# One DiT layer on one core: the array fed during the first loads, S5's two directions in one scan, and an order with a place for each instruction

## The chip, the core and the metric

The kernel runs on one core of a Trainium2 chip: TensorE (PE, with its weight loads as PEld), VectorE (DVE), ScalarE (ACT), GpSimd (POOL) and the queue that issues the transfers (SP) each work through their own list of instructions in order, and wait on each other through semaphores. The metric is the device time of one execution in microseconds; lower is better.

## The reference, cut to what matters

One layer over 512 latent tokens and a prefix of 256 context tokens, 1024 channels, all float32.

```
h   = rms_norm(x) * (1 + scale) + shift        # scale, shift, gate from silu(c) @ W_ada
prj = h @ W_in     # q,k,v | GLA q,k,v,gates | S5 input (256) | three merge gates (3 x 1024)
A = bidirectional gated linear attention, chunks of 64 tokens
B = bidirectional S5: 16 groups of 16 channels, 64 complex states each
    state_t = a * state_{t-1} + B u_t, once forward in time and once backward; y = Re(C state) + D u
C = grouped-query softmax attention, 4 heads over context + latent keys
m = sum_i sigmoid(gate_i) * (branch_i @ W_br_i);  x += gate * (m @ W_out)
x += gate2 * ffn(rms_norm(x) * (1 + scale2) + shift2)    # 2816 wide, width-3 convolution
```

## The kernel before

Everything is recorded first and ordered afterwards. A class `Sched` stands in for the engines: each call (`PE.matmul`, `V.tensor_tensor`, `SY.dma_start`) is recorded as an operation with its cost in a model, its predecessors, and the name of the part that was current (`part("s5z0")`). `prepare` gives every operation a rank: the longest chain behind it, but at least the number that the table `WANT` has for its part. `forward` then walks through model time and gives each engine, whenever it is free, the ready operation of the highest rank. `emit` writes the real instructions in that order, so one line number stands for all of them (L408). What the chip does with the list is then fixed: an engine whose next instruction has to wait holds up everything behind it. Copies recorded on `VS` or `VG` may be placed on DVE or on ACT or POOL, as the planner finds room.

Float32 products are taken as three passes over split operands (`hh`/`hl` high and low part of the normalised input, `wbgh`/`wbgl` of a weight), hence three matmuls of 128x512 for each tile. The casts that make the parts run on ACT, DVE and POOL.

The stages, in the order of time. **Start**: 12 matmuls of ones (`warm`); the input in 8 tiles `xT`; their mean square (`rl`); and for each of 8 blocks of channels k a `modulation(k)`: 2 tiles `ada` of 512 KB, 8 matmuls that fill a quarter of the array's columns each, a copy `adar`, 2 small matmuls, then scale and shift, from which `hh`, `hl` are made. **b1**: the projection of block k as soon as its `hh` stands (`b1a`, `b1c`). `low` is the projection to GLA's gates (`tp<-hh,wgl`, 96x512). **S5**: the 16 groups in four quarters q; each turns its input (`uT`, copied to `U`), multiplies it into the state space (`Z`), rotates it by tables `co`, `si` (`zt`, `z`), scans along 512 columns (`so`), rotates back (`x_`) and multiplies into `y`. The rows of `Z` from 0 to 63 are forward states, 64 to 127 backward states; the scan runs left to right on the first half and right to left on the second, as two instructions:

```python
V.tensor_tensor_scan(xo[0:64, 1:512], df[0:64, 0:511], zf[0:64, 0:511], 0.0, ...)
V.tensor_tensor_scan(xo[64:128, 0:511][:, ::-1], df[64:128, 1:512][:, ::-1], zf[64:128, 1:512][:, ::-1], 0.0, ...)
```

**Attention** (`sc`, `sl` scores; `sm` their maximum; `Pc`, `Pl` exponentials; `pt`, `ptc` transposes; `oatt`), **GLA** (`tp`, `kvE`, `kvO`, `ba`, `bo`), **output and residual** (`tk`, `h2T`) and the **FFN** (`up`, `tk`) follow. Two sorts of work are free to stand nearly anywhere from b1 to the residual: the merge gates `bg` (576 matmuls of 128x512, whose weights come in 24 tiles `wbg`) and the branch outputs `br`. The planner lays them where PE would otherwise wait.

Of the kernel before, what the change touches and what calls it, by code (L numbers as in the profile page):

```python
# [15 lines left out]
ALU = mybir.AluOpType  # L16
# [12 lines left out]
NWARM = 12  # L29
WHOLE = ("mm8t",)  # L30
# [4 lines left out]
SHARE = 0.97  # L35
WANT = {
# [87 lines left out]


class _Op:
    __slots__ = ("i", "alts", "acc", "succ", "npred", "news", "fset", "mcost", "part", "pe", "port")


class Sched:  # L130
# [1791 lines left out]
```

## Time and profile before

| what | value |
|---|---|
| median of 3 runs | 942.54 us (935.72 to 943.57) |
| the profiled execution | 944.47 us, of which 942.7 us are its span |
| PE busy | 887.6 us, 94% |
| DVE, ACT, POOL busy | 606.6, 376.7, 169.8 us |
| moved by DMA | 107.67 MB, 114 GB/s on the mean |

Times in the trace are microseconds from the start of the span. A stretch in which PE is busy at a granted clock of 1.0 is at full speed; at 0.5 the same matmuls take twice as long and PE still counts as busy. So the busy share alone doesn't say where time is lost: the granted clock is read beside it.

### The profile page before, as it was taken

Reading aid. Unit: us, or ns where it says so; the run is one execution under the profiler, and the core shown is the slowest. Engines: PE = TensorE matmul, PEld = TensorE weight load, DVE = VectorE, ACT = ScalarE, POOL = GpSimd, SP = SyncE. Lnnn points to the kernel's source line nnn. Section 1 sums busy time; section 2 is a strip of 40 time slices with the busy share of each in tenths; the row PEclk is TensorE's granted clock in tenths of the full one; section 3 lists DMA queues with packets and bytes.
Section 4 is the critical chain, followed back from the end, with each engine's and each line's share of the span. In section 5 each row is a group of like instructions: output and inputs, shape, how many; then the busy total and the mean of one; then the engine's idle time right before and its main releaser. Section 6 shows DMA issues by size and latency. Waiting matters only on the chain.

```text
span 942.7 us, 12225 instructions
## 1 busy us (share of the span) xinstructions
PE 887.6 (94%) x4552; PEld 716.3 (76%) x4552; DVE 606.6 (64%) x1151; ACT 376.7 (40%) x710; POOL 169.8 (18%) x132
## 2 busy tenths in 40 slices
PE   6999986789999999999899989999999999999996
PEld 4597864567777888778788767888888888888885
DVE  7679789987768432495644787454575546956314
ACT  4445154355754633244364375122232223722001
POOL 2310020003221432167056402110100100100000
PEclk7599996889999999999999997999999999999999
DMA  9715112140224322356447312222232222443101
GB/s 339 296 62 180 50 50 66 52 165 25 89 68 143 112 67 90 113 200 201 146 166 257 129 34 81 87 90 67 90 126 98 90 67 85 162 147 128 60 23 68
DMA packets 39644, 107.67 MB, mean 114 GB/s; under 512 B 7214, under 2 KB 10942, under 8 KB 39584
## 3 DMA queue, kind: packets, MB, share of 16 engines
q1 hardware_dynamic: 39584, 106.88, 33.5%
q8 instruction: 36, 0.59, 0.3%
q14 instruction: 24, 0.20, 0.1%
HBM read 103.49 MB, written 3.38 MB: 113 GB/s over the span
## 4 chain that ended last, share of the span: by engine, by line
PE 49%; DVE 5%; DMA 1%; issue 1%; ACT 0%; DVEq 0%; SPq 0%
PE up L408 26%; PE tk L408 15%; PE bg L408 4%; PE br L408 2%; PE tp L408 1%; DVE so L408 1%; DMA wbg<-in_wbg 1%; DVE x L408 1%; DVE tmp L408 0%; DMA ada<-in_ada 0%; PE bo L408 0%; DVE rsx L408 0%; DVE y L408 0%; DVE ml L408 0%; DVE rsy L408 0%
## 5 line engine op out<-in xcount | busy, mean ns | idle before, releaser
L408 PE MATMUL up<-h2h,wuph 128*128 128x512 f32 (+1 forms) x384 | 118.5, 377 | 2.5 <-ACT h2h L408 2.5
L408 PE MATMUL up<-h2h,wupl 128*128 128x512 f32 (+1 forms) x384 | 114.5, 374 | 0.0
L408 PE MATMUL up<-h2l,wuph 128*128 128x512 f32 (+1 forms) x384 | 114.5, 375 | 0.0
L408 PE MATMUL bg<-hh,wbgh 128*128 128x512 f32 x192 | 79.2, 425 | 9.5 <-ACT wbgh L408 5.6
L408 PEld LDWEIGHTS up<-h2h,wuph 128*128 128x128 f32 x384 | 70.6, 190 | 17.0 <-ACT h2h L408 3.2
L408 PEld LDWEIGHTS up<-h2h,wupl 128*128 128x128 f32 x384 | 70.5, 189 | 14.5 <-DVE wupl L408 0.5
L408 PEld LDWEIGHTS up<-h2l,wuph 128*128 128x128 f32 x384 | 70.5, 190 | 12.6 <-POOL h2l L408 0.2
L408 PE MATMUL bg<-hh,wbgl 128*128 128x512 f32 x192 | 77.8, 421 | 1.1 <-DVE wbgl L408 1.1
L408 PE MATMUL bg<-hl,wbgh 128*128 128x512 f32 x192 | 77.7, 418 | 0.0
L408 ACT CAST wuph<-wup 128x1024 fp32r<-128x1024 f32 x26 | 27.4, 1054 | 119.1 <-PE up L408 106.2
L408 DVE CAST wuph<-wup 128x1024 fp32r<-128x1024 f32 x18 | 11.9, 691 | 82.4 <-PE up L408 80.1
L408 DVE SCALAR_TENSOR_TENSOR u<-up,col,u 128x511 f32<-128x511 f32 x88 | 60.0, 742 | 3.8 <-ACT u L408 3.6
L408 POOL TENSOR_TENSOR wupl<-wup,wuph 128x1024 fp32r<-128x1024 f32 x9 | 21.6, 2407 | 215.2 <-ACT wuph L408 169.1
L408 POOL TENSOR_TENSOR j<-ada,cbc 128x1024 f32<-128x1024 f32 x16 | 39.6, 2483 | 101.4 <-DMA ada<-in_ada 39.4
L408 PEld LDWEIGHTS bg<-hh,wbgh 128*128 128x128 f32 x192 | 38.0, 198 | 21.0 <-ACT wbgh L408 7.5
L408 PE MATMUL tk<-wtkl,gh 128*128 128x512 f32 x176 | 51.5, 390 | 0.0
L408 PE MATMUL tk<-wtkh,gh 128*128 128x512 f32 x176 | 51.5, 389 | 0.0
L408 PE MATMUL tk<-wtkh,gl 128*128 128x512 f32 x176 | 51.4, 389 | 0.0
L408 DVE TENSOR_TENSOR wupl<-wup,wuph 128x1024 fp32r<-128x1024 f32 x35 | 41.1, 1219 | 15.7 <-PE up L408 14.5
L408 PEld LDWEIGHTS bg<-hh,wbgl 128*128 128x128 f32 x192 | 37.2, 194 | 11.2 <-DVE wbgl L408 2.3
L408 DVE TENSOR_TENSOR wtkl<-wtk,wtkh 128x1024 fp32r<-128x1024 f32 x22 | 26.6, 1221 | 28.4 <-PE tk L408 13.9
L408 PEld LDWEIGHTS bg<-hl,wbgh 128*128 128x128 f32 x192 | 37.4, 195 | 8.9 <-issue 0.5
(483 smaller groups left out, 2009.9 us busy)
## 6 DMA issues: line engine op xcount, KB each, us to landing
ada<-in_ada SPq DMA_DIRECT2D x48, 512.0 KB, 4.9
wup<-in_wup SPq DMA_DIRECT2D x44, 512.0 KB, 3.5
wbg<-in_wbg SPq DMA_DIRECT2D x24, 512.0 KB, 4.4
wtk<-in_wdn SPq DMA_DIRECT2D x22, 512.0 KB, 5.1
wP<-in_wP SPq DMA_DIRECT2D x16, 512.0 KB, 4.0
wbr<-in_wbr SPq DMA_DIRECT2D x8, 512.0 KB
wo<-in_wout SPq DMA_DIRECT2D x16, 256.0 KB, 4.2
w<-in_wB SPq DMA_DIRECT2D x8, 384.0 KB, 7.8
```

Source lines behind the costliest of these rows:

```text
L408: r = getattr(self.real[e], m)(*a, **k)
```

## The change

Three things. (1) Before each of the first loads is used, PE multiplies it by ones: 2 matmuls of 128x128 on each of the 8 `xT` tiles and 1 on each `ada` tile of the first two blocks, 20 in all, into an accumulator that nobody reads. All `modulation(k)` are recorded ahead of the loop over `h`. (2) S5's backward direction gets its input in reversed order of the columns (`R`, two more copies for each quarter), so both directions run left to right: 64 `Z` matmuls in two halves of the columns instead of 32 whole ones, one scan of 128 rows instead of two of 64, and `x_` is put together in two halves, the second written in reverse. (3) `WANT` has a number for each instruction of a part (in units of 50 ns) where it had one for the part, and the rank of an operation is held to its own number; the rule that gave all of a part `mm8t` one rank is gone, and some constants of the model are other ones.

```diff
-NWARM = 12
-WHOLE = ("mm8t",)
+NWARM, NWX, NWA, KWA = 12, 2, 1, 2
...
 WANT = {
-    "": -540.5, "start": -775.6, "warm": 1508.5, "xT": -852.4, "ada0": 973.9, "h0": 896.3, "b10": 763.6, "ada1": 897,
...
+    "h0": [2038, 1563, 1399],
...
 def prepare(self):
-            r = self.want.get(o.part, 0.0) * 1000.0
+            at = self.want.get(o.part)
+            r = -50.0 * at[o.k] if at else 0.0
...
-        top = {}
-        for o in ops:
-            if o.part.startswith(WHOLE):
-                top[o.part] = max(top.get(o.part, 0.0), rank[o.i])
-        return [top.get(o.part, rank[o.i]) for o in ops]
+        return rank
...
-    part("warm")
-    b = ps("warm")
-    for _ in range(NWARM):
-        PE.matmul(b[:, 0:P], lhsT=onesm, rhs=onesm, start=True, stop=True)
+    accA = [ps("b1a") for _ in range(4)]
+    accC = [ps("b1c") for _ in range(2)]
+
+    def warm(src, n):
+
+        at, sc.part_ = sc.part_, "warm"
+        for _ in range(n):
+            PE.matmul(accC[1][:, 0:P], lhsT=onesm, rhs=src[:, 0:P], start=True, stop=True)
+        sc.part_ = at
+
+    warm(onesm, NWARM)
...
         SY.dma_start(t, A["xT"][k])
         xT.append(t)
+        warm(t, NWX)
...
             SY.dma_start(w, A["ada0"][k, i])
+            if k < KWA:
+                warm(w, NWA)
...
+    for k in range(KT):
+        modulation(k)
     for k in range(KT):
         part(f"h{k}")
         hi, lo = g2("hh", dt=F32R), g2("hl", dt=F32R)
-        modulation(k)
-        part(f"h{k}")
...
         VS.copy(U[:, :, 96:128], b3[:, :, 0:32])
+        R = g2("R", [P, 4, 128])
+        VS.copy(R[:, :, 32:128], b3[:, :, 0:96][:, :, ::-1])
+        VS.copy(R[:, :, 0:32], b3[:, :, 0:32][:, :, ::-1])
...
-                PE.matmul(b[:, j * P:j * P + P], lhsT=pT[i][:, j * P:j * P + P], rhs=U[:, j, :], start=True, stop=True)
+                for d, x in enumerate((U, R)):
+                    PE.matmul(b[64 * d:64 * d + 64, j * P:j * P + P], lhsT=pT[i][:, j * P + 64 * d:j * P + 64 * d + 64],
+                              rhs=x[:, j, :], start=True, stop=True)
...
-            V.tensor_tensor_scan(xo[0:64, 1:512], df[0:64, 0:511], zf[0:64, 0:511], 0.0, op0=ALU.mult, op1=ALU.add)
-            V.tensor_tensor_scan(xo[64:128, 0:511][:, ::-1], df[64:128, 1:512][:, ::-1], zf[64:128, 1:512][:, ::-1],
-                                 0.0, op0=ALU.mult, op1=ALU.add)
+            V.tensor_tensor_scan(xo[:, 1:512], df[:, 0:511], zf[:, 0:511], 0.0, op0=ALU.mult, op1=ALU.add)
...
-            if i == 0:
-                mul(x_, so[0], cl)
-                mul(x2, so[1], sl)
-                sub(x_, x_, x2)
...
+            mul(x1, so[0], (cl, sl)[i])
+            mul(x2, so[1], (sl, cl)[i])
+            (sub, add)[i](x_[0:64], x1[0:64], x2[0:64])
+            (sub, add)[i](x_[64:128, :, ::-1], x1[64:128], x2[64:128])
...
-    c["kidx"] = np.where(dirn == 0, s, 127 - s)
-    c["kmask"] = np.where(dirn == 0, s != 0, s != 127)
+    c["kidx"] = s + 0 * dirn
+    c["kmask"] = (s != 0) + 0 * dirn
```

The order that comes out of the new table differs nearly everywhere. Three places show it. In these lists a name ends in a buffer's number, shapes are those of what is written, and x4 is four in a row.

On PE at the start, before: the modulation's matmuls stand in a row, and the projection `b1a` of block 0 follows them.

```order
L408 MATMUL ada_161<-ada_95_162,cpad_75 32x256 x4
L408 MATMUL ada_161<-ada_96_163,cpad_75 32x256 x4
L408 MATMUL ada_171<-ada_105_172,cpad_75 32x256 x4
L408 MATMUL ada_161<-cst_68,adar_164 128x2 x2
L408 MATMUL ada_171<-ada_106_173,cpad_75 32x256 x4
L408 MATMUL ada_180<-ada_114_181,cpad_75 32x256 x4
L408 MATMUL ada_171<-cst_68,adar_174 128x2 x2
L408 MATMUL b1a_106<-w1h_119,hh_112 128x512
L408 MATMUL b1a_108<-w1h_119,hh_112 128x512
L408 MATMUL b1c_110<-w1h_119,hh_112 128x256
```

On PE at the start, changed: the same matmuls, and `low` (`tp_233`) of the blocks already normalised between them.

```order
L919 MATMUL tp_233<-hh_148,wglh_231 96x512
L919 MATMUL ada_123<-ada_58_125,cpad_75 32x256 x4
L919 MATMUL ada_127<-ada_62_129,cpad_75 32x256 x4
L919 MATMUL ada_123<-cst_68,adar_126 128x2 x2
L919 MATMUL tp_233<-hl_149,wglh_231 96x512
L919 MATMUL tp_233<-hh_148,wgll_232 96x512
L919 MATMUL ada_127<-cst_68,adar_130 128x2 x2
L919 MATMUL tp_233<-hh_154,wglh_231 96x512
L919 MATMUL tp_233<-hl_155,wglh_231 96x512
L919 MATMUL tp_233<-hh_154,wgll_232 96x512
L919 MATMUL ada_131<-ada_66_133,cpad_75 32x256 x4
```

What moved: 19 of the 24 matmuls of `low` now stand ahead of the first `b1a` and the other five just behind it; before they stood around the `Z` of S5's second quarter, together with the context's 24 of 96x256, which have left S5 too.

On DVE in S5's second quarter, before (the scan is listed as SCALAR_TENSOR_TENSOR): two rotations, four scans, and `x_` in three steps for each half of the complex number.

```order
L408 TENSOR_TENSOR zt_359<-zt_359,z_289_361 128x512
L408 TENSOR_TENSOR zt_358<-zt_358,z_288_360 128x512
L408 SCALAR_TENSOR_TENSOR so_291_363<-d_283_355,zt_359 64x511
L408 SCALAR_TENSOR_TENSOR so_290_362<-d_283_355,zt_358 64x511 x2
L408 SCALAR_TENSOR_TENSOR so_291_363<-d_283_355,zt_359 64x511
L408 TENSOR_TENSOR x__292_364<-so_290_362,co_354 128x256
L408 TENSOR_TENSOR x_293_365<-so_291_363,si_353 128x256
L408 TENSOR_TENSOR x__294_366<-so_290_362,si_353 128x256
L408 TENSOR_TENSOR x__292_364<-x__292_364,x_293_365 128x256
L408 TENSOR_TENSOR x_295_367<-so_291_363,co_354 128x256
```

On DVE at the same place, changed.

```order
L919 TENSOR_TENSOR zt_362<-zt_362,z_292_364 128x512
L919 TENSOR_TENSOR zt_361<-zt_361,z_291_363 128x512
L919 SCALAR_TENSOR_TENSOR so_294_366<-d_286_358,zt_362 128x511
L919 SCALAR_TENSOR_TENSOR so_293_365<-d_286_358,zt_361 128x511
L919 TENSOR_TENSOR x_297_369<-so_294_366,si_356 128x256
L919 TENSOR_TENSOR x_296_368<-so_293_365,co_357 128x256
L919 TENSOR_TENSOR x__295_367<-x_296_368,x_297_369 64x256
L919 TENSOR_TENSOR x__295_367<-x_296_368,x_297_369 64x4x64
```

What moved: two scans of 128 rows stand where four of 64 rows stood; and each `x_` is written by two instructions of 64 rows.

On PE in the attention, before: scores with the merge gates `bg` between them.

```order
L408 MATMUL sc_578<-kTc_507,qT_505 128x256 x4
L408 MATMUL sl_581<-kTl_506,qT_505 128x512
L408 MATMUL sl_582<-kTl_506,qT_505 128x512
L408 MATMUL bg_652<-hl_132,wbgh_650 128x512
L408 MATMUL sl_581<-kTl_506,qT_505 128x512
L408 MATMUL sl_582<-kTl_506,qT_505 128x512
L408 MATMUL bg_652<-hh_131,wbgl_651 128x512
L408 MATMUL bg_652<-hh_140,wbgh_650 128x512
L408 MATMUL bg_652<-hl_141,wbgh_650 128x512
```

On PE in the attention, changed.

```order
L919 MATMUL sc_578<-kTc_518,qT_516 128x256 x4
L919 MATMUL br_490<-ol_465,wbrh_472 128x512
L919 MATMUL br_490<-oh_464,wbrl_473 128x512
L919 MATMUL pt_574<-cst_68,Pl_573 128x128 x3
L919 MATMUL ptc_566<-cst_68,Pc_561 128x128 x4
L919 MATMUL pt_576<-cst_68,Pl_575 128x128 x4
L919 MATMUL pt_565<-cst_68,Pl_564 128x128 x2
L919 MATMUL sl_592<-kTl_517,qT_516 128x512 x2
L919 MATMUL sl_593<-kTl_517,qT_516 128x512 x2
L919 MATMUL br_515<-oh_462,wbrh_497 128x512
L919 MATMUL br_515<-ol_463,wbrh_497 128x512
L919 MATMUL br_515<-oh_462,wbrl_498 128x512
```

What moved: the branch outputs `br` stay, but the `bg` are mostly gone from here. Of the 576 matmuls of `bg`, the list before has 56 ahead of S5's first `uT`, 143 from there to its last `y`, 185 in the attention, none up to GLA's first `kvO`, and 192 behind it; the changed list has 48, 264, 48, 48 and 168 at the same places.

## Rows read from the trace of the kernel before

**Rows 1.** The page: busy time, share and instructions of each engine.
```profile
PE 887.6 (94%) x4552; PEld 716.3 (76%) x4552; DVE 606.6 (64%) x1151; ACT 376.7 (40%) x710; POOL 169.8 (18%) x132
```

**Rows 2.** Stretches: start:end, length, busy (count) by engine, clock, DMA share, GB/s.
```profile
12.00:26.00 14.00, 8.46 (x44) 5.43 (x44) 13.26 (x42) 7.02 (x11) 2.06 (x3) 0.50 1.03 408
26.00:41.00 15.00, 13.47 (x98) 6.82 (x97) 9.46 (x23) 6.63 (x13) 4.21 (x10) 0.50 0.96 371
...
103.60:206.60 103.00, 81.02 (x467) 61.28 (x466) 94.36 (x158) 43.32 (x74) 6.53 (x7) 0.84 0.27 83
206.60:324.00 117.40, 116.41 (x633) 91.36 (x631) 86.51 (x188) 72.28 (x160) 28.40 (x26) 1.00 0.24 79
...
393.50:477.00 83.50, 76.49 (x484) 63.12 (x480) 61.56 (x147) 33.72 (x81) 37.17 (x19) 0.98 0.49 164
...
560.00:575.00 15.00, 10.59 (x43) 7.49 (x44) 14.96 (x54) 13.98 (x39) 5.63 (x7) 0.70 0.24 72
575.00:935.00 360.00, 360.00 (x1670) 299.10 (x1669) 195.47 (x275) 99.28 (x142) 16.86 (x7) 1.00 0.28 94
```

**Rows 3.** PE in order of time, first 52 us: start, length, names, count, idle before.
```profile
1.05 5.42 PE L408 MATMUL warm<-onesm 128*128 128x128 f32 x24 [1.05 <-DVE onesm L408]
7.86 0.64 PE L408 MATMUL ada<-ada,cpad 128*32 128x256 f32 x8 [1.39 <-DMA ada<-in_ada]
...
38.98 1.93 PE L408 MATMUL ada<-ada,cpad 128*32 128x256 f32 x16
40.84 1.01 PE L408 MATMUL ada<-cst,adar 128*128 128x2 f32 x4
41.72 1.20 PE L408 MATMUL b1a<-w1h,hh 128*128 128x512 f32 x2
...
50.22 0.59 PE L408 MATMUL b1a<-w1h,hh 128*128 128x512 f32 x1
...
52.03 0.39 PE L408 MATMUL b1a<-w1h,hh 128*128 128x512 f32 x1
52.26 0.39 PE L408 MATMUL b1a<-w1h,hl 128*128 128x512 f32 x1
```

**Rows 4.** The tile `ada` to 50 us: issues (ns; first and last start).
```profile
L408 SPq DMA_DIRECT2D ada<-in_ada x16: 328/328/432, 2.1 to 24.1; - x16
```

**Rows 5.** Transfers to 50 us: KB each, median us from issue to landing.
```profile
ada<-in_ada SPq DMA_DIRECT2D x16, 512.0 KB, 9.2
```

**Rows 6.** DVE by groups, 103.6 to 206.6: count, busy us, mean ns, idle before.
```profile
L408 DVE TENSOR_TENSOR_SCAN so<-d,zt 64x511 f32<-64x511 f32 x16 | 19.0, 1209 | 0.3
L408 DVE TENSOR_TENSOR wbgl<-wbg,wbgh 128x1024 fp32r<-128x1024 f32 x6 | 7.1, 1212 | 0.0
...
L408 DVE TENSOR_TENSOR zt<-Z,co 128x512 f32<-128x512 f32 x8 | 5.1, 684 | 8.1 <-PE Z L408 4.5 <-ACT co L408 3.6
...
L408 DVE TENSOR_TENSOR x<-so,si 128x256 f32<-128x256 f32 x4 | 1.7, 418 | 0.0
...
L408 DVE TENSOR_TENSOR lowT<-tp,lowT 32x512 fp32r<-32x512 f32 x1 | 0.7, 689 | 0.0
```

**Rows 7.** The clock in one gap of S5, same columns as Rows 2.
```profile
150.00:167.00 17.00, 12.51 (x54) 8.86 (x55) 16.01 (x29) 11.01 (x18) 0.00 (x0) 0.51 0.21 65
```

**Rows 8.** `bg` on PE by stage: stretch, length, busy us (count), clock, DMA.
```profile
103.60:206.60 103.00, 38.28 (x136) 0.84 0.27 83
206.60:324.00 117.40, 53.81 (x186) 1.00 0.24 79
```

**Rows 9.** DVE and ACT by groups, 206.6 to 324: the attention's softmax.
```profile
L408 DVE TENSOR_REDUCE sm<-sl 128x1 f32<-128x512 f32 x16 | 10.5, 681 | 1.6 <-PE sl L408 1.5
...
L408 ACT ACTIVATE Pl<-sl,sm 128x512 f32<-128x512 f32 x16 | 11.1, 692 | 6.3 <-DVE sm L408 5.8 <-PE ptc L408 0.5
...
L408 ACT COPY PTl<-pt 128x512 f32<-128x512 f32 x10 | 5.8, 588 | 6.5 <-PE bg L408 2.8 <-PE oatt L408 1.7 <-PE pt L408 1.5
```

**Rows 10.** ACT by groups, the whole span: the table loads.
```profile
L408 ACT ACT_TABLE_LOAD x22 | 28.2, 1283 | 6.0 <-PE suf L408 4.0 <-DVE u L408 0.9 <-PEq L1912 0.7
```

More of the change, by code (lines that the diff above doesn't have):

```diff
@@ L36 @@
 WANT = {
[51 rows of a table removed]
+    "": [-9977, 71, 1824],
+    "start": [3753, 2271, 3056, 3913, 3778, 4646, 4819, 3704],
+    "warm": [3309, 3365, 3316, 2747, 3811, 3514, 2773, 3144, 2920, 3004, 2910, 3102, -458, -562, -735, -789, -1374,
[37 rows of a table added]
+    "evac": [475],
[99 rows of a table added]
+    "rope": [4907, 5877],
+    "ssq": [1766, 1821, 2006, 1909, 1924, 2072, 3030],
[69 rows of a table added]
+    "gln": [8196, 8206, 8217, 8238, 8227, 8248, 9902, 8268, 8307, 8356, 8325, 8381],
[39 rows of a table added]
+    "mask": [-495, -870, -122, 64, 3570, 3580],
[26 rows of a table added]
+    "sso": [9475, 9507, 9512, 9538, 9542, 9546, 9550],
[4 rows of a table added]
+    "cbc": [4442, 5286, 5343, 5595],
[280 rows of a table added]
 }
@@ L126 @@
 class _Op:
-    __slots__ = ("i", "alts", "acc", "succ", "npred", "news", "fset", "mcost", "part", "pe", "port")
+    __slots__ = ("i", "k", "alts", "acc", "succ", "npred", "news", "fset", "mcost", "part", "pe", "port")
 class Sched:
@@ L156, in __init__ @@
         self.want = {}
+        self.count = {}
     def part(self, name):
@@ L237, in _pe @@
         else:
-            w, c, y = max(4.0 * n / 2.4 + 8.0, 224.0), max(4.0 * n / 1.2, 240.0), max(4.0 * n, 256.0)
+            w, c, y = max(4.0 * n / 2.4 + 8.0, 224.0), max(4.0 * n / 1.2, 440.0), 4.0 * n
         nr = 1 if rows <= 32 else 2 if rows <= 64 else 4
@@ L246, in _pe @@
                 cells |= 1 << (4 * r + q)
-        return w, c, cells, y * rows / 128.0, 8 * nr + nc_, kind
+        return w, c, cells, y, 8 * nr + nc_, kind
     def _port(self, eng, m, aps_w, aps_r):
@@ L265, in _cost @@
             run = min(self._run(x) for x in aps_w + aps_r)
-            return n * out.shape[0] * 4 / (360.0 if run >= 128 else 180.0)
+            return n * out.shape[0] * 4 / (390.0 if run >= 128 else 180.0)
         if eng == "PE":
@@ L353, in record @@
         o.part = self.part_
+        o.k = self.count[self.part_] = self.count.get(self.part_, -1) + 1
         o.pe = self._pe(m, aps_w[0], k["lhsT"] if "lhsT" in k else a[1]) if "PE" in engs else None
@@ L416, in array @@
             return max(st, was[2] + 28.0)
+        if was[1] == 1 and pe[5] == 0:
+            return max(st, max(cell) + 88.0)
         if pe[4] != was[0]:
@@ L454, in forward @@
         actset = None
-        sent = [0.0] * 7
-        tick, cols, warm = 0, 0.0, False
+        sent = [0.0] * 6 + [4100.0]
+        tick, cols, warm = 0, [0.0] * 16, False
         cell = [0.0] * 16
@@ L554, in forward @@
                 if t_ != tick:
-                    warm = t_ == tick + 1 and cols >= 3060.0
-                    tick, cols = t_, 0.0
-                cols += o.pe[3]
+                    warm = t_ == tick + 1 and max(cols) >= 3060.0
+                    tick, cols = t_, [0.0] * 16
                 c = o.pe[0 if warm else 1]
@@ L562, in forward @@
                         cell[q] = st + c
+                        cols[q] += o.pe[3]
             end = st + c
@@ L816, in modulation @@
         V.tensor_scalar(gate_s[:, 0, k, :], b[:, 256:258], adabc[:, k:k + 1], None, op0=ALU.add)
-    accA = [ps("b1a") for _ in range(4)]
-    accC = [ps("b1c") for _ in range(2)]
+    for k in range(KT):
+        modulation(k)
     for k in range(KT):
@@ L1177, in record @@
         for i in range(2):
-            x_, x2 = g2("x_", [P, 4, 64]), g2("x2", [P, 4, 64])
-            if i == 0:
-                mul(x_, so[0], cl)
-                mul(x2, so[1], sl)
-                sub(x_, x_, x2)
-            else:
-                mul(x_, so[0], sl)
-                mul(x2, so[1], cl)
-                add(x_, x_, x2)
+            x_, x1, x2 = (g2(n_, [P, 4, 64]) for n_ in ("x_", "x1", "x2"))
+            mul(x1, so[0], (cl, sl)[i])
+            mul(x2, so[1], (sl, cl)[i])
+            (sub, add)[i](x_[0:64], x1[0:64], x2[0:64])
+            (sub, add)[i](x_[64:128, :, ::-1], x1[64:128], x2[64:128])
             xs.append(x_)
```

603 rows, old and new, of the table WANT are left out of this document.

## The prediction

> **What bounds the kernel now.** I read the busy shares first. PE is busy for 94% of the span [rows 1], so there seem to be 55 us to win. That is too little, because a PE at half clock also counts as busy. The table of stretches with the granted clock says more [rows 2]. From 575 to 935 us PE works without a gap at full clock: 360 us that only fewer matmuls could shorten, and the change leaves that list as it is. What is lost lies ahead of it, in two places above all.
>
> The first is the start. From 12 to 41 us the clock is at its lower level, 1.2 GHz (0.50), first while PE waits for loads (8.46 us busy of 14), then with PE nearly full (13.47 of 15) [rows 2]. In order of time the modulation's `ada` matmuls follow each other at the end, so PE sets the pace there, not the transfers; the first `b1a` stands at 41.72 us, and the spacing halves only after 50.22 us [rows 3]. The last `ada` tile was issued at 24.1 us and a tile took 9.2 us to land [rows 4, 5], so by about 33 us all of them were there.
>
> The second is S5, from 103.6 to 206.6 us: PE is busy 81.02 of 103.00 us at a mean clock of 0.84, DVE 94.36 [rows 2]. DVE is the bound. PE waits for it, and in the gaps the clock drops: 150 to 167 us is nearly all at the lower level [rows 7]. I put the loss at 22.0 us idle, plus 12 for half speed (the clock is low for (1 - 0.84) x 2 x 103 = 33 us, PE is busy in about three quarters of that as in rows 7, and half of this is lost): 34 us; 69 us of work at full clock were done. The attention behind it loses 1 us, the output of GLA 7, the residual 4.4 and some clock [rows 2].
>
> **The change part by part.** I sum against the profiled execution, 944.5 us (942.7 of span, 1.8 around it); the median of the runs is 1.9 below it.
>
> *The start.* A matmul of 512 columns takes 0.23 us at full clock (52.03 to 52.26) [rows 3], twice that at half. Ahead of the first `b1a` the changed list has 20 more matmuls of ones, 19 of `low`, and the `ada` work of one more tile with its two small matmuls. The yardstick is the moment at which `b1a` could have started with the full clock: before, 41.72 plus half of the 8.9 us up to the rise, so 46.2 us. If the clock stays low, the order adds 19 x 0.46 = 8.7 us, about 2 for the `ada` work (0.97 and 0.94 from the rows at 38.98 and 40.84), and 2 for the four of ones among the `ada`; the other sixteen fill the wait for `xT`. With a part of the 7 us idle from 12 to 41 us filled, `b1a` starts at 51 to 53 us, which is worth 53 to 55 on the yardstick: 8 us later, and 24 x 0.23 = 5.5 us of `low` done early. The sum is a loss of 2.5 us. If the clock is high throughout, PE is never late, and the last `ada` tile decides: 33 us plus its matmuls (two tiles took 2.7 us from 38.98 to 41.72 at the low clock) and, as an estimate, as long again for its copy and scale: 38 us, 8 us earlier, 5.5 of `low` on top, less some 3 us for a projection that then waits for its inputs: a gain of 11. I take a gain of 5, nearer to the first end, because the stretch from 26 to 41 us shows what this mixture does: PE 90% busy, with matmuls that fill a quarter of the columns, and the clock stayed at 0.50 [rows 2, 3]. Between them there is now `low`, yet less of it than `ada`; and behind the matmuls on `xT` PE still waits for the mean square.
>
> The Trainium skill (TensorE: Matmul & The Clock Gate, "What's actually happening") says that the lower clock is the default and that PE's recent activity releases it. By this rule alone the fed array would have the full clock from the first loads on, and the result would be the first rival. The trace agrees in part: the matmuls behind the 12 of ones took 0.64 us for eight at 7.86, against 0.97 later [rows 3]; but 13.47 busy us of 15 released nothing.
>
> *S5.* On DVE 16 scans of 1209 ns go and 8 of twice the rows come [rows 6]. Rows cost nothing in this trace as far as it shows: 32x512 took 689 ns, 128x512 684 [rows 6]. So a scan of 128x511 should stay near 1.21 us: 9.7 us saved; at worst it takes twice as long, and nothing is saved. The halves of `x_` add 8 x 0.42 = 3.4 us [rows 6]. The rest of the saving is not left free: in the changed list three more `wbgl` (1212 ns each), one more `wbrl`, two casts and five steps of the attention's preparation stand between the first `zt` and the last `x_`. Row by row at the durations of the trace DVE has 89 us there, 91 before. So S5 takes nearly as long as it did, 100 us instead of 103, but PE has more to do in it: 120 more `bg` (264 for 144), 27 us; 24 of `low`, 24 of the context's `low` at half the columns and 23 of `b1a` go, 13.5 us. That is 83 us at full clock, so that 14 to 17 us stay idle, where 34 were lost; the clock costs nothing while PE has such slack. I take 20 us of gain; between 10 (scans at double price) and 30 (DVE's idle 8.6 us gone as well). The copies `R`, eight on ACT at some 0.6 us, lie in ACT's idle time (43 of 103 us busy) [rows 2].
>
> *Attention.* The `bg` spent in S5 are missing here: 48 for 186 [rows 8]. PE has about 59 us left, and DVE 62 to 64 in the changed list, plus what a softmax takes from score to product. Before, 1.0 us was idle [rows 2]. PE will wait 5 to 10 us, so I take 5 us of loss; the bounds are 0 and 20, the latter if the clock drops here as it did in S5.
>
> *GLA, output, residual.* `bg` is 168 for 183 behind `kvO`, and DVE has 43 us for PE's 33 in the worst part, so the 7 us idle between 393.5 and 477 [rows 2] go only in part: a gain of 3 (from 6 to a loss of 3). ACT has five more table loads at 1283 ns [rows 10], 6.4 us, next to 50 idle us in this stage. The residual has the same chain as before in the same order; its 15 us with 10.59 busy [rows 2] stay. Transposes and matmuls alternate less: 1 us.
>
> The sum: 5 + 20 - 5 + 3 + 1 = 24 us, so 920.5 us for a profiled execution and 918.6 for the median.
>
> **The rivals.** *The clock is held at the start.* For it: the matmuls of ones did raise the clock at 6 to 8 us, and the planner now has work for each gap. Against it: rows 2 and 3 as above. It is worth 6 to 9 us more: 910 us.
>
> *S5 is paid back in the attention.* PE's list there holds softmax work whose inputs come from DVE and ACT, with little between; the waits of S5 move here, with the clock's fall. Against it: `br` is still there, and scores stand far ahead of their transposes. At the upper bound of 20 us the time is 934.
>
> *Slower, by one mechanism: PE in order behind the softmax.* Each of 16 blocks takes 0.68 us for `sm`, 0.69 for `Pl`, 0.59 for the copy `PTl` [rows 9] and about as much again in small steps and handing on, 3 us. If PE stood through each of them, 48 us would be lost. It decides from a wait of (24 + 5) / 16 = 1.8 us for each block on, beyond which the gain is gone; at 3 us the time is 961. Against it: in the list some 80 rows of PE lie between a score and its transpose.
>
> *The scan is not cheaper.* With 128 rows at double price S5 keeps 10 us more: 929.
>
> **How the numbers follow.** The forecast of 918.6 gets 0.47, the held clock 0.25, the payback 0.15, the dear scan 0.07, the slower case 0.06. The range reaches from 892, a held clock with S5's idle time gone (910 - 10) and the attention and GLA at their lower bounds (5 and 3 less), to 940, the payback with half of the dear scan on top; outside lie the slower case and the ends of the others. A measurement of this kernel can tell about 1% from no change, 9.4 us. Faster than 933.1: nearly all of the forecast and of the first rival, half of the payback, most of the dear scan: 0.80. Within 1%: 0.13. Slower: 0.07.
>
> **What the profile would show.** The start: the first `b1a` at 38 to 40 us at full clock (rival) or near 50 (low clock). S5: eight scans near 1.21 us, DVE busy above 90% from the first `zt` to the last `x_` in 93 to 97 us, `bg` for most of PE's time, idle PE 14 to 17 us. Attention: DVE above 85% busy, PE idle 5 to 10 us. From the first `up` behind the residual to the end, 368 to 372 us as before. Wrong would make me: a wait in S5 for something other than DVE (`wbgh` of ACT, a late `wbg`), or a clock that falls where PE has no slack.

## The result and the profile after

The changed kernel takes 915.79 us in the median of four runs (914.41 to 921.17); the kernel before, run beside it, 942.17 us (935.72 to 943.57). The ratio is 0.974, with a 95% interval from 0.969 to 0.979. The forecast was 918.6 us in a range from 892 to 940. The profiled execution took 921.17 us with 919.4 of span; it is the slowest of its kernel's runs, and the spans of its other executions lie between 912.5 and 914.9 us. Against the 942.7 us of the profiled span before, 23.3 us are gone; the prediction's sum had 24. Between the medians lie 26.4 us.

The page of the kernel after: busy time, share and instructions by engine, and the granted clock in 40 slices, in tenths.

```profile
PE 878.5 (96%) x4656; PEld 713.5 (78%) x4656; DVE 627.0 (68%) x1174; ACT 381.0 (41%) x713; POOL 163.6 (18%) x119
...
PEclk9999999899999999999999989999999999999999
```

PE is busy for 9 us less than before though it has 104 more matmul records, and DVE for 20 us more [rows 1]. The first says that less of PE's busy time was at half clock. Where, the stretches tell. Their edges have moved with the stages: start, S5 (from the first `uT` to the first `y5T`), attention (to the first `dctx`), residual, and what follows it. Columns: start:end, length, busy (count) of PE, PEld, DVE, ACT, POOL, granted clock, DMA share, GB/s. The short one inside S5 answers to the gap of [rows 7].

```profile
12.00:26.00 14.00, 12.17 (x114) 8.09 (x112) 13.85 (x51) 5.38 (x10) 0.00 (x0) 0.93 1.01 394
26.00:41.00 15.00, 13.30 (x108) 7.04 (x107) 13.75 (x38) 6.69 (x12) 4.32 (x6) 1.00 1.03 399
103.70:207.00 103.30, 94.36 (x610) 72.79 (x608) 94.91 (x172) 48.43 (x90) 7.70 (x4) 0.93 0.33 106
...
150.00:175.00 25.00, 20.99 (x122) 16.06 (x119) 21.64 (x35) 11.12 (x19) 2.38 (x1) 0.80 0.37 118
...
207.00:277.00 70.00, 63.74 (x372) 47.86 (x371) 66.39 (x156) 49.72 (x123) 24.38 (x26) 1.00 0.20 69
...
553.00:912.60 359.60, 359.60 (x1670) 298.69 (x1668) 205.81 (x273) 98.27 (x138) 28.82 (x12) 1.00 0.28 93
```

In [rows 2] S5 begins with the first `Z`, 2.3 us behind the first `uT`, and the attention ends 4.2 us ahead of the first `dctx`. Cut as here, the two stages of the kernel before are:

```profile
101.30:206.60 105.30, 83.32 (x479) 63.15 (x478) 94.36 (x158) 43.97 (x76) 6.53 (x7) 0.84 0.26 81
206.60:328.20 121.60, 120.61 (x651) 94.67 (x650) 87.52 (x189) 74.03 (x162) 32.60 (x30) 1.00 0.25 84
```

Four things are to be seen. At the start the clock is 0.93 and 1.00 where it was 0.50 twice [rows 2]. S5 takes 103.3 us for 105.3, but PE has 610 matmul records in it instead of 479, at a clock of 0.93 instead of 0.84, and 8.9 us idle instead of 22.0. The attention, which took 121.6 us, is over after 70. And from 553 us on nothing has changed: from there to the end of the span it is 366.4 us, and 367.7 before (942.7 less 575), with 1670 matmul records in the gapless part of both.

So the gain doesn't show in S5's own length: S5 is 2 us shorter and holds what stood elsewhere. To compare like with like I priced each matmul of the two lists at the spacing that it has at full clock without a wait, and took what a stage lasted beyond this as lost. Lost time goes from 35.6 to 22.9 us ahead of S5, from 33.8 to 16.7 in S5, from 3.6 to 11.5 in the attention, and in the rest (the transposes behind it, GLA, output, residual and end) from 41.2 to 38.0. That makes 25.1 us; the list itself is 1.8 us longer, and 23.3 stay. These are estimates, since no row has the prices: with the mean spacing of each sort of matmul instead, the four differences are 16, 18, -8 and 5 us, against a list that is 8 us longer. What both say alike is that S5 gives most, the start second, and that the attention loses about 8.

PE at the start, in order of time (start, length, names, count, idle before):

```profile
9.08 5.47 PE L919 MATMUL b1c<-xT,onesm 128*128 128x128 f32 x32 [2.53 <-DMA xT<-in_xT]
...
16.55 1.07 PE L919 MATMUL ada<-ada,cpad 128*32 128x256 f32 x16
...
40.54 0.74 PE L919 MATMUL b1a<-w1h,hh 128*128 128x512 f32 x2
```

The matmuls of ones on `xT` are the first row. Sixteen records of `ada` take 1.07 us, where [rows 3] had 1.93 for as many, and the first `b1a` stands at 40.54 us at full clock (0.74 for two, 1.20 before).

The DVE groups of S5 (103.7 to 207; count, busy us, mean ns, idle before):

```profile
L919 DVE TENSOR_TENSOR wbgl<-wbg,wbgh 128x1024 fp32r<-128x1024 f32 x8 | 9.7, 1217 | 0.8 <-ACT wbgh L919 0.8
...
L919 DVE TENSOR_TENSOR_SCAN so<-d,zt 128x511 f32<-128x511 f32 x8 | 9.3, 1202 | 0.0
```

Eight scans of 128 rows take 1202 ns each, sixteen of 64 rows had taken 1209 [rows 6]: 9.7 us are saved, and `wbgl` alone takes up 2.6 us of them (9.7 for 7.1). DVE as a whole is at 94.91 us, as full as before. What PE does in the stage is told by `bg`, in S5 and in the attention:

```profile
103.70:207.00 103.30, 65.06 (x264) 0.93 0.33 106
207.00:277.00 70.00, 11.21 (x43) 1.00 0.20 69
```

It was 136 (144 from the first `uT`) and 186 [rows 8]. The attention's 70 us are then nearly bare, and PE idles 6.3 us there, where it idled 1.0; the longest of its waits (us in total, times, longest):

```profile
PE glu L919 <- ACT y5T L919: 1.7, 1, 1.7
PE ptc L919 <- ACT Pl L919: 1.5, 1, 1.5
```

Followed back from its end, the chain of work that ended last runs through DVE without a break from 219.5 to 239.8 us. Two pieces of that stretch, and a third one at 248.8 us, are instructions of one column (`sm`, a step of the softmax) that take ten to fifteen times what they take otherwise. The first two as pieces of the chain (start, us); POOL and DVE in order of time; and all `sm` of this form (count, ns min/median/max, first and last start), changed and before:

```profile
228.64 2.20 DVE sm L919 x2
235.84 2.27 DVE sm L919
```

```profile
228.42 2.38 POOL L919 TENSOR_TENSOR wbrl<-wbr,wbrh 128x1024 fp32r<-128x1024 f32 x1 [9.16 <-ACT wbrh L919]
228.62 2.21 DVE L919 TENSOR_TENSOR sm<-sm 128x1 f32<-128x1 f32 x1
235.68 2.40 POOL L919 TENSOR_TENSOR j<-ada,cbc 128x1024 f32<-128x1024 f32 x1 [3.08 <-issue]
235.84 2.26 DVE L919 TENSOR_TENSOR sm<-sm 128x1 f32<-128x1 f32 x1
```

```profile
L919 DVE TENSOR_TENSOR sm<-sm x24: 140/152/2261, 223.2 to 268.4; 128x1 f32<-128x1 f32 x16, 128x2 f32<-128x2 f32 x8
L408 DVE TENSOR_TENSOR sm<-sm x24: 140/153/217, 235.4 to 276.0; 128x1 f32<-128x1 f32 x16, 128x2 f32<-128x2 f32 x8
```

The third takes 1.61 us at 248.77, beside POOL's of 247.98 (2.38 us). Each of the three starts while POOL works on a tile of 128x1024 and ends within 0.03 us of POOL's instruction. Together they cost DVE 5.6 us of the 66.4 that it counts as busy in this stage. In the attention before, no `sm` met such an instruction, and the longest took 0.217 us.

### The profile page after: what moved, and what is told of

It is laid out like the page before. It is cut to its first block, busy times and chain, and to the rows that moved or that the text cites. A ratio compares the mean times of both kernels' runs of the same rounds, so it can differ in the third digit from the quotient of the medians.

```text
span 919.4 us, 12381 instructions
## 1 busy us (share of the span) xinstructions
PE 878.5 (96%) x4656; PEld 713.5 (78%) x4656; DVE 627.0 (68%) x1174; ACT 381.0 (41%) x713; POOL 163.6 (18%) x119
## 4 chain that ended last, share of the span: by engine, by line
PE 75%; DVE 13%; DMA 4%; issue 3%; ACT 2%; POOL 2%; SPq 0%; DVEq 0%; POOLq 0%; ACTq 0%
PE up L919 27%; PE tk L919 15%; PE bg L919 11%; PE tp L919 9%; PE br L919 4%; DMA ada<-in_ada 3%; PE b1a L919 2%; DVE sm L919 2%; DVE so L919 1%; PE b1c L919 1%; PE oatt L919 1%; DVE r L919 1%; PE pt L919 1%; DVE i L919 1%; DMA xT<-in_xT 1%
## 5 line engine op out<-in xcount | busy, mean ns | idle before, releaser
L919 PE MATMUL up<-h2h,wuph 128*128 128x512 f32 (+1 forms) x384 | 137.3, 376 | 3.8 <-ACT h2h L919 3.3
L919 PE MATMUL up<-h2l,wuph 128*128 128x512 f32 (+1 forms) x384 | 136.6, 374 | 0.0
L919 PE MATMUL up<-h2h,wupl 128*128 128x512 f32 (+1 forms) x384 | 135.0, 374 | 0.0
L919 PEld LDWEIGHTS up<-h2h,wuph 128*128 128x128 f32 x384 | 72.9, 190 | 17.1 <-ACT h2h L919 3.6
L919 ACT ACTIVATE u<-up,col 128x512 f32<-128x512 f32 x44 | 33.6, 778 | 93.3 <-PE up L919 93.3
L919 DVE SCALAR_TENSOR_TENSOR u<-up,col,u 128x511 f32<-128x511 f32 x88 | 64.2, 746 | 10.1 <-ACT u L919 8.9
L919 POOL TENSOR_TENSOR wupl<-wup,wuph 128x1024 fp32r<-128x1024 f32 x12 | 30.2, 2524 | 191.8 <-PE up L919 151.1
L919 PE MATMUL tk<-wtkh,gl 128*128 128x512 f32 x176 | 62.1, 389 | 0.0
L919 PE MATMUL tk<-wtkl,gh 128*128 128x512 f32 x176 | 61.8, 390 | 0.0
L919 PE MATMUL tk<-wtkh,gh 128*128 128x512 f32 x176 | 60.9, 390 | 0.0
L919 DVE SCALAR_TENSOR_TENSOR th<-th,u 128x512 f32<-128x512 f32 x44 | 35.3, 809 | 12.8 <-ACT th L919 12.2
```

What stands on the lines that cost most here:

```text
L919: r = getattr(self.real[e], m)(*a, **k)
```

## The experiments

Each ratio is to the kernel before, run on the same chip in turn with it, with a 95% interval. Times of stages are from one profiled execution of each kernel: the first `uT` opens S5, the first `y5T` closes it, the first `dctx` closes the attention.

### Is it the matmuls of ones that keep the clock up?

**The changed kernel without the 20 matmuls of ones on the loads** (nobody reads their result).

```diff
             m, a, k, _ = self.ops[i].alts[e]
+            if self.ops[i].part == "warm" and self.ops[i].k >= 12:
+                continue
```

> The changed kernel in its own order, with the 20 matmuls of ones on the first loads left out (the 12 at the very start stay); nothing of the result depends on them. Theory: they hold TensorE's clock through the first loads, so without them it falls while PE waits for the mean square and stays low until the projection is dense; the first b1a moves from 40.5 us to 48 to 53 us and the time from 915.8 to 922 to 928 us. Rival: the start was won by the earlier gates (low) and the order of the loads; then the clock is no lower from 26 to 41 us than with them, and the time is 911 to 917 us.

Measured: 916.93 us, ratio 0.9745 (0.9707 to 0.9783), the changed kernel's time. The first `b1a` stands at 40.3 us, the first `uT` at 102.0. PE from 14 us on and the two stretches around the rise:

```profile
14.08 1.86 PE L921 MATMUL rl<-onesm,ssum 128*128 128x1 f32 x8 [8.73 <-DVE ssum L921]
15.87 3.64 PE L921 MATMUL ada<-ada,cpad 128*32 128x256 f32 x32
19.44 1.88 PE L921 MATMUL rl<-dg,onesm 128*128 128x128 f32 x8
21.15 0.51 PE L921 MATMUL ada<-cst,adar 128*128 128x2 f32 x4
```

```profile
15.00:20.00 5.00, 5.00 (x39) 2.72 (x40) 5.00 (x24) 0.64 (x2) 0.00 (x0) 0.50 1.03 407
20.00:26.00 6.00, 5.71 (x55) 3.65 (x53) 5.38 (x17) 2.06 (x4) 0.00 (x0) 0.92 1.03 410
```

PE idles 8.73 us ahead of 14 us, and what follows starts at the lower clock (3.64 us for 32 records of `ada`). The clock rises all the same, near 21 us: four records of `adar` take 0.51 us where [rows 3] have 1.01. Before it stand four `ada` tiles in a row and eight records of `rl`. The clock came up without the feed.

**Both once more, on one chip: the changed kernel as it is, and the one without the ones.** No edit in the first, the edit above in the second.

> The changed kernel once more, as the measure for the others of this call: 914 to 917 us by both theories.

> The changed kernel without the 20 matmuls of ones on the first loads once more, beside the changed kernel on one chip. In one profile of this start the clock stayed high from 21 us on, in another (with the weights on POOL) it fell again at 27 us and b1a came 4 us later. Theory: the feed makes the clock of the first loads sure, and without it some executions lose 3 to 6 us: 916.5 to 920 us, a wider spread than with it. Rival: the feed does nothing: the same median within 1 us.

Measured: 914.41 us, 0.974 (0.9707 to 0.9773), with them, and 914.62 us, 0.9743 (0.9709 to 0.9776), without. The 20 matmuls make no difference that these runs can show. The changed kernel's S5 and attention in this execution:

```profile
100.70:200.70 100.00, 91.46 (x611) 71.02 (x609) 95.01 (x173) 48.42 (x90) 7.73 (x4) 0.97 0.35 110
200.70:270.60 69.90, 63.64 (x371) 47.79 (x371) 66.28 (x156) 49.72 (x123) 24.39 (x26) 1.00 0.20 70
```

The 100.0 us of S5 and its idle 8.5 are nearer to what the kernel usually does than the 103.3 of the first profile; without the ones S5 took 100.7.

**The run of `ada` matmuls broken.** Without the ones on the loads, and with two matmuls of 128x2 (like the two behind each `adar`) put behind each of the first four `ada` tiles, into the accumulator that nobody reads.

```diff
+            if self.ops[i].part == "warm" and self.ops[i].k >= 12:
+                continue
...
+            if self.ops[i].part == "warm":
+                tiny = (a[0][:, 0:2], k["lhsT"], k["rhs"][:, 0:2])
+            elif e == "PE" and self.ops[i].part.startswith("ada") and a[0].shape[0] == 32:
+                runs += 1
+                if runs in (4, 8, 12, 16):
+                    for _ in range(2):
+                        self.real["PE"].matmul(tiny[0], lhsT=tiny[1], rhs=tiny[2], start=True, stop=True)
```

> The changed kernel in its own order without the 20 matmuls of ones on the first loads, and with two small matmuls (128x2) behind each of the first four ada tiles, as before's list had them there: about 4 us more work on PE at the low clock, at a place where transfers still set the pace. Theory: without the feed the clock rose at about 20.5 us, behind four ada tiles in a row; broken up they don't raise it, the mixture of ada, adar and low stays at the low clock to the projection, b1a starts at 46 to 52 us instead of 40.3 and the time is 922 to 930 us. Rival: low among the ada matmuls raises the clock all the same: b1a at 40 to 43 us, 915 to 920 us.

Measured: 922.54 us, 0.9798 (0.9763 to 0.9832), 6 to 8 us behind the two kernels without the ones. The first `b1a` stands at 49.0 us, the first `uT` at 110.8. PE in order of time, then two stretches:

```profile
17.98 1.01 PE L929 MATMUL b1c<-onesm 128*128 128x2 f32 x4
...
37.89 0.61 PE L922 MATMUL ada<-cst,adar 128*128 128x2 f32 x4
```

```profile
20.00:26.00 6.00, 6.00 (x35) 4.36 (x35) 2.26 (x10) 0.37 (x1) 0.00 (x0) 0.50 1.02 410
26.00:33.00 7.00, 7.00 (x46) 3.99 (x46) 4.87 (x15) 1.84 (x4) 0.07 (x1) 0.50 1.03 406
```

Four us of extra work at the low clock (each pair stands for 1.01 us) come between the `ada` tiles, PE is then 100% busy from 20 to 33 us, and the clock stays at the lower level until 37.8 us: the picture of the kernel before [rows 2, 3]. So a PE without idle time may stand at 1.2 GHz. Of the 9 us by which `uT` is later, 6 to 8 reach the end. But the run changes two things at once: where the unbroken row had the low clock by itself (the run with casts on ACT, below, 0.50 from 20 to 33 us), the first `b1a` stood at 44.8 us. By that measure about half of the 8.7 us by which `b1a` is later here is the clock, and the other half the four pairs' own 4 us. Nor does the run show that the row of tiles is what raises the clock: see the run with S5's new code alone, at the end.

**The feed alone, in the kernel before.** The 20 matmuls of ones come in, and their accumulator is allocated earlier; `modulation` is still recorded inside the loop, and table and rule are those of the kernel before. With this order the accumulator of the ones is already in use when some of them run, so that a part of the running projection `b1c` is overwritten.

```diff
-NWARM = 12
+NWARM, NWX, NWA, KWA = 12, 2, 1, 2
...
+        warm(t, NWX)
...
+            if k < KWA:
+                warm(w, NWA)
```

> The kernel before, with the 20 matmuls of ones on the first loads and the two accumulators allocated earlier, ordered by its own planner; low stays in S5. Theory: the fed array has the full clock for a part of the first loads, but from the third block on only quarter-array matmuls are left, so the clock falls again before the projection: the first b1a at 38 to 42 us, and the time 934 to 940 us. Rival: what keeps the clock up is low between the modulation's matmuls, and feeding alone does nothing: 940 to 944 us. Other rival: feeding alone is enough, b1a starts at 37 us at full clock: 932 to 934 us.

Measured: 941.01 us, 1.0024 (0.999 to 1.0059): nothing. Yet its trace shows the first `b1a` at 23.3 us, 18 earlier than before. The granted clock is .50, .78, .91 and .79 in the stretches 15 to 20, 20 to 26, 26 to 33 and 33 to 41 us, and the first `uT` stands at 99.1 us for 101.3. S5 ends at 206.8 us for 206.6. So the first `b1a` is a poor measure here: of its 18 us only 2 are left at `uT`, and S5 takes these back, with DVE busy for 94.5 us as before (94.4) and waiting 2 us more. The early start was worth nothing here.

### Is S5 set by DVE?

**Each scan as two, rows 0 to 63 and 64 to 127**, so that DVE has the old number of scans, 9.7 us more, and all else is as changed.

```diff
+            if m == "tensor_tensor_scan":
+                for h in (slice(0, 64), slice(64, 128)):
+                    r = getattr(self.real[e], m)(*(x[h] if j < 3 else x for j, x in enumerate(a)), **k)
+                continue
```

> The changed kernel in its own order, with each of S5's 8 scans issued as two, on rows 0 to 63 and on rows 64 to 127: the same numbers, 8 more scans at 1.2 us on DVE, 9.7 us. Theory: S5 is bound by DVE, which is 92% busy there, so S5's last y comes 6 to 10 us later, the idle time of PE in S5 grows by as much, and the time is 922 to 926 us. Rival: with so many merge-gate matmuls PE has become the bound there and DVE has slack; then the time is 915 to 918 us.

Measured: 928.27 us, 0.9869 (0.983 to 0.9907), 12 to 14 us slower than the changed kernel. The stage and the scans (count, ns min/median/max, first and last start):

```profile
103.10:213.90 110.80, 93.37 (x611) 71.74 (x609) 105.33 (x181) 48.63 (x90) 7.74 (x4) 0.95 0.32 102
```

```profile
L921 DVE TENSOR_TENSOR_SCAN so<-d,zt x16: 1203/1216/1220, 111.5 to 206.8; 64x511 f32<-64x511 f32 x16
```

DVE's busy time rises by 10.3 us over the repeated run, and the stage by 10.8 us: one for one. PE has the same 611 records, and its idle time there rises from 8.5 to 17.4 us. The other 2.4 us of the two spans' difference lie ahead of S5 (`uT` at 103.1 for 100.7). DVE is the bound, and the halved scan count is worth about the 9.7 us that it takes out.

**Four of S5's eight `wbgl` from DVE to POOL.** `low` are the `wbgl` of `bg` that the order gives to DVE and that POOL can do as well.

```diff
+        self.pool_ = {low[j] for j in (3, 5, 7, 9)}
...
+            if i in self.pool_:
+                e = "POOL"
```

> The changed kernel in its own order, with four of the eight low halves of the merge gates' weights (wbgl) that stand on DVE in S5 given to POOL, which is busy 8 of 103 us there: DVE has 4.9 us less. Theory (S5 bound by DVE): S5's last y comes 3 to 5 us earlier and the time is 910.5 to 913.5 us. Rival: POOL takes 2.4 us for each where DVE takes 1.2, PE waits for them or DVE is slowed beside POOL, and nothing is won: 915 to 920 us.

Measured: 920.6 us, 0.9782 (0.9749 to 0.9815), 5 to 6 us slower and not faster. POOL in order of time, the scans and `win` on DVE, and the stage:

```profile
110.35 3.17 POOL L924 TENSOR_TENSOR wbgl<-wbg,wbgh 128x1024 fp32r<-128x1024 f32 x1 [4.93 <-ACT wbgh L924]
125.76 8.50 POOL L924 TENSOR_TENSOR wbgl<-wbg,wbgh 128x1024 fp32r<-128x1024 f32 x1 [12.24 <-ACT wbgh L924]
134.94 2.40 POOL L924 TENSOR_TENSOR wbgl<-wbg,wbgh 128x1024 fp32r<-128x1024 f32 x1 [0.68 <-DVE wbgh L924]
```

```profile
L924 DVE TENSOR_TENSOR_SCAN so<-d,zt x8: 1189/1214/3349, 110.1 to 199.8; 128x511 f32<-128x511 f32 x8
L924 DVE SCALAR_TENSOR_TENSOR win<-cst,col,win x4: 226/232/2320, 105.2 to 186.7; 128x16 f32<-128x16 f32 x4
```

```profile
101.70:207.20 105.50, 93.66 (x611) 72.93 (x609) 95.57 (x169) 48.42 (x90) 26.06 (x8) 0.95 0.33 104
```

DVE has four instructions of 1.22 us fewer in the stage (169 for the repeat's 173), 4.9 us, but its busy time is 95.57 us where it was 95.01: one scan took 3349 ns, in the pair that started at 110.11 us, beside POOL's instruction of 110.35, and one `win` of 16 columns 2320 ns, at 186.66 us beside POOL's of 184.65 (4.30 us). These two took back 2.1 us each, a table step (`i`) and the casts 0.9 between them. POOL's own took from 2.4 to 8.50 us. So DVE was not relieved at all, and waited 5 us more besides (9.9 us idle for 5.0); for the longer waits the rows give no single cause. The Trainium skill (SBUF — State Buffer, "Who interferes with whom") says that a DVE instruction with two inputs in SBUF contends with a GpSimd instruction that reads SBUF; scan and `wbgl` both have two such inputs, and these rows agree.

**Both edits together: without the ones, and with the four `wbgl` on POOL.**

> The changed kernel in its own order without the 20 matmuls of ones on the first loads and with four of the wbgl of S5 on POOL. Theory: the first does nothing (916.9 us against 915.8), the second relieves DVE in S5: 910 to 914 us. Rival: no gain from POOL, 915 to 920 us.

Measured: 920.93 us, 0.9784 (0.9754 to 0.9813). Again 5 to 6 us are lost to POOL (here an `x` of 256 columns took 2552 ns for 418). In its profiled execution, which begins with the same four `ada` tiles in a row, the clock fell again, to 0.76 from 26 to 33 us and 0.57 from 33 to 41; `b1a` stood at 44.1 us.

**Three casts `wbgh` of S5 from DVE to ACT**, which has half of the stage idle.

```diff
+        self.act_ = set(hs[:3])
...
+            if i in self.act_:
+                e = "ACT"
```

> The changed kernel in its own order, with the three high halves of the merge gates' weights (wbgh) that DVE casts within S5 given to ACT, which is busy 48 of 103 us there; DVE has 2.1 us less work and doesn't stand for a late weight (1.7 us of its idle time in S5). Theory (S5 bound by DVE, and ACT doesn't disturb it as POOL did): S5's last y comes 2 to 4 us earlier, the time is 911 to 914 us. Rival: ACT then stands for the weight with S5's copies and tables behind it, and S5 gets longer: 916 to 922 us.

Measured: 917.19 us, 0.9767 (0.9734 to 0.98): no gain. S5 took 101.8 us, and DVE is busy for 94.92 of them although 2.1 us were taken from it. The rows show where they went: one `zt`, at 168.58 us, met a `wbgl` that POOL has in the changed kernel too, and took 1.8 us more.

```profile
L924 DVE TENSOR_TENSOR zt<-zt,z x8: 679/682/2466, 114.1 to 199.4; 128x512 f32<-128x512 f32 x8
168.11 2.39 POOL L924 TENSOR_TENSOR wbgl<-wbg,wbgh 128x1024 fp32r<-128x1024 f32 x1 [26.89 <-ACT wbgh L924]
```

So neither this run nor the one with POOL gave DVE less to do in S5, and neither speaks against DVE as the bound. Here, too, the profiled execution has a late clock, although the ones are in:

```profile
20.00:26.00 6.00, 6.00 (x38) 3.51 (x37) 3.22 (x10) 1.58 (x3) 0.00 (x0) 0.50 1.03 410
```

Nothing ahead of 26 us was edited, and the same stretch of the changed kernel had 1.00. So the start's clock also differs between executions of the same list. The Trainium skill (TensorE: Matmul & The Clock Gate, "What's actually happening") says that one kernel can show different numbers of slow matmuls in different runs; these two traces agree.

### What binds the attention?

**Seven scalings of `Pl` on DVE left out** (those that POOL could do as well; 3.6 us; the softmax weights stay unnormalised there).

```diff
+        self.out_ = {i for _, _, i, e in order if e == "DVE" and "POOL" in self.ops[i].alts
+                     and any(r[0].startswith("Pl") for r, wr in self.ops[i].acc if wr)}
...
+            if i in self.out_:
+                continue
```

> The changed kernel in its own order, with the seven scalings of attention weights (Pl) that stand on DVE left out, 3.6 us of DVE; these weights stay unnormalised. Theory: the attention, short of merge gates now, is bound by DVE (66 of 70 us busy), so its end comes 2.5 to 3.5 us earlier and the time is 912 to 913.5 us. Rival: it waits for the way from score to product, through ACT and the copies, and DVE's work decides nothing: 914.5 to 917 us.

Measured: 915.47 us, 0.9751 (0.9718 to 0.9783), and the stage:

```profile
204.20:273.70 69.50, 63.65 (x371) 47.83 (x371) 63.73 (x149) 49.72 (x123) 23.33 (x26) 1.00 0.20 70
```

DVE has 2.6 us less to do and the attention takes 69.5 us for 69.9 to 70.0. These scalings don't set it. They all stand late in the stage (from 252.2 us on in the first profile), behind the stretch in which the chain runs through DVE, so the run doesn't test that stretch; its three long `sm` are there again (2.2, 2.2 and 1.6 us).

### Is it the code or the order?

**S5's new code in the kernel before**, with the old table, one number for each part.

```diff
+        R = g2("R", [P, 4, 128])
...
+                for d, x in enumerate((U, R)):
...
+            V.tensor_tensor_scan(xo[:, 1:512], df[:, 0:511], zf[:, 0:511], 0.0, op0=ALU.mult, op1=ALU.add)
...
+            (sub, add)[i](x_[0:64], x1[0:64], x2[0:64])
```

> The kernel before, with S5's part of the change alone (reversed copy, one scan for both directions, x_ in halves), ordered by its own planner with one place for each part. Theory: DVE has about 6 us less to do in S5 and nothing new is laid there, so S5 gets 3 to 7 us shorter and the time falls from 942 to 935 to 939 us. Rival: this code is what won S5's 17 us; then the time is 923 to 928 us.

Measured: 955.84 us, 1.018 (1.0127 to 1.0234): slower than before, and outside what either theory gave. S5 lasts from 94.8 to 221.2 us; the stage, and the longest wait of DVE in it:

```profile
94.80:221.20 126.40, 98.61 (x616) 73.56 (x614) 104.98 (x194) 50.88 (x105) 13.97 (x11) 0.84 0.22 68
```

```profile
DVE qk L408 <- PE b1a L408: 14.3, 1, 14.3
```

With the old numbers the planner laid the end of b1 inside S5 (last `b1a` at 108.2 us), and DVE stood 14.3 us before a `qk` that needed it. In the kernel before, `b1a` reaches into S5 too, to 117.6 us, but no instruction of DVE waited for it there. The run is confounded in that the table was made for other instructions; what the code would be worth with a table of its own in the old form wasn't tried.

Its start answers another question. The first 364 records of PE are those of the kernel before, one by one: no ones on the loads, no `low`, `ada` and `adar` in turn. PE in order of time:

```profile
25.04 1.94 PE L408 MATMUL ada<-ada,cpad 128*32 128x256 f32 x16
27.52 0.61 PE L408 MATMUL ada<-cst,adar 128*128 128x2 f32 x4 [0.55 <-DVE adar L408]
28.06 1.07 PE L408 MATMUL ada<-ada,cpad 128*32 128x256 f32 x16
36.40 0.72 PE L408 MATMUL b1a<-w1h,hh 128*128 128x512 f32 x2
```

The clock is up by 27.5 us, and the first `b1a` stands at 36.4 us for 41.7 [rows 3]. So the old order can have the high clock as well, in some executions, and the new one the low clock (the two above with `b1a` at 44.1 and 44.8). Neither the ones nor the order of the tiles decides it alone. Of the nine profiled executions with the changed order at the start, unbroken, with the ones or without, seven have the high clock from 26 us to the first `b1a`; of the two with the old order, one has it.

**The changed kernel with the mean of a part's numbers for all its instructions.**

```diff
-            r = -50.0 * at[o.k] if at else 0.0
+            r = -50.0 * sum(at) / len(at) if at else 0.0
```

> The changed kernel with one place for each part again (the mean of the places of its instructions), ordered anew by its planner. Theory: the code of S5 and the fed array by themselves win little, and the gain is in which instructions stand in DVE's list in S5; with means that list is no longer matched, and the time is 935 to 965 us. Rival: the parts' places carry the order and the places within a part are detail: 914 to 922 us.

Measured: 1105.3 us, 1.1763 (1.1713 to 1.1812), over 140 us beyond what either theory gave. From 100 to 200 us:

```profile
100.00:200.00 100.00, 31.38 (x219) 21.84 (x217) 57.81 (x105) 20.94 (x47) 13.91 (x11) 0.57 0.08 22
```

PE is busy for 31 us of 100, no engine is full, and transfers run at 22 GB/s. The means of this table are no usable order; they don't show what a good table of the old form would do, but they show that the gain hangs on the places.

## Why the prediction was right, and where not

**The sum.** 24 us were forecast and 23.3 measured in the profiled spans, 918.6 us forecast and 915.79 measured in the median. That the two sums meet within a microsecond is in part luck: by the lost times above the start gave 3.4 us more than forecast, S5 2.9 less, the attention lost 2.9 more, and the rest gave 1.7 more with a list that is 2.5 us shorter without the ones (17.1 + 8.4 - 7.9 + 3.2 + 2.5 = 23.3). The profiled execution of the changed kernel is also its slowest; the repeat's span is 911.7 us, with the first `uT` 3.0 us and S5's end 6.3 us earlier.

**S5: right in its mechanism, 17 us for 20.** The step was that DVE bounds the stage, that the cheaper scan makes room which is filled again, and that `bg` takes PE's idle time. Each part shows: scans of 1202 ns on 128 rows, so the dear-scan rival falls; DVE at 92% of the stage, which lasts 100.4 us from the first `Z` (106.6 us), as the forecast's 100 for 103 is counted; 264 `bg` in it. Lost time on PE is 16.7 us, forecast as 14 to 17 us idle; in the first profile about half of it is idle (8.9 us) and half is clock, which I had put at nothing: 0.93 on the mean and 0.80 from 150 to 175 us. The start of that sum, 34 us lost before, agrees with the 33.8. The experiment with the scans in halves adds the proof: 10.3 us more on DVE, 10.8 us more of S5.

**The start: the wrong picture, and a number near the middle.** The two ends were -2.5 and 11 us. The sum took 5 and called it nearer to the low-clock end; it is in fact just past the middle (4.25). The picture behind it was the low clock, with the first `b1a` near 50 us, because "the mixture" of `ada`, `adar` and `low` had not raised the clock before. The clock was up by 15 us, `b1a` stood at 40.5, and the lost time fell by 12.7 us, of which 4.3 are the ones' own 20 matmuls at some 0.21 us (half of the 5.42 / 12 at the low clock [rows 3] gives 0.23), taken as work of the longer list: 8.4 us, nearer to the second end; priced by the mean spacing it is some 3 us more. The first rival had this picture, but for the wrong reason. It put the clock down to the ones, and these are worth nothing (914.41 with them, 914.62 without). What the step missed is that one list can have either clock: it took the one profile before, with its low clock, for what the mixture does. The old order has the high clock in one of its two traces (`b1a` at 36.4 us), the new one the low clock in two of nine. In a trace like the former, the start before would have lost some 5 us less (36.4 for 41.7), and less of the gain would lie here. What decides the clock, and how often each order gets it, stays open.

**The attention: 8 us lost for 5.** PE idles 6.3 us, within the forecast 5 to 10, and DVE is 95% busy, as "above 85%" said. But part of DVE's time isn't the work that I had counted (62 to 64 us): three `sm` of one column stand beside POOL's `wbrl` and `j` and take 5.6 us more than such instructions do. The first two lie on the chain in the stretch where it runs through DVE (219.5 to 239.8 us); behind it the chain changes between PE, DVE and ACT, with PE's waits at most 1.7 us. What the stage would take without the three wasn't tried, and the run without the scalings took its work from a place off that stretch. The rivals of payback (20 us) and of PE behind the softmax don't show.

**The rest.** GLA, output, residual and end lost 3.2 us less with the transposes, for 4 forecast with the order's 1. Behind `kvO` the forecast reckoned with 168 `bg` for 183; the list before had 192 there. The FFN's 368 to 372 us were said to run from the first `up`; from there it is 375.8 us (543.6 to 919.4) and was 377.7 before (565.0 to 942.7). The forecast's figure fits the gapless part and what follows it, 366.4 for 367.7 us. That it stays as it was is right.

**Faster or not.** Nothing that was tried beats the changed kernel: DVE's work in S5 given to POOL cost 5 to 6 us and given to ACT won nothing, and the two kernels at 914.6 and 915.5 us are within its own runs.

## What to carry to other kernels

Find the engine that sets a stage before moving work: in the stage that DVE sets here, PE took 131 more matmul records in no more time. Time won ahead of such a stage may be lost in it (2 us, in the run with the feed alone), but time lost ahead of it came through here (9 us at `uT`, 6 to 8 at the end, in the run with the broken row). Two passes over half the partitions, joined into one over all of them, halve the time where the rows cost nothing, and the gain then appears where the freed engine's stage takes in work from others, not as a shorter stage. A second engine with room to spare is no relief by itself; add up the first one's durations afterwards, instruction by instruction, because a held-up instruction counts as busy. And take a second trace of the kernel before, too, before a clock that one trace shows goes into a forecast.

## What the runs showed of the hardware that was not expected

- Of seven `wbgl` of 128x1024 on POOL in S5 four took 2.36 to 2.41 us and three 3.17, 4.30 and 8.50; the mean was 3647 ns, three times DVE's 1217. A DVE scan beside one took 3349 ns for 1214.
- A DVE instruction can be held up whatever its size: an `sm` of one column took 2.21 us for 0.15 beside a POOL instruction of 2.38 us and ended 0.03 us behind it, and a `win` of 16 columns 2.32 us for 0.23. The profile counts this as busy.
- With PE busy for 13 of 13 us (20 to 33 us) the granted clock stayed at 0.50 where 128x2 matmuls stood between the `ada` tiles. The same list of PE had 0.50 from 26 to 33 us in one execution and 0.91 in another (kernel before, and the run with S5's new code alone), and the changed list 1.00 and 0.50.
